# A two-block sequence model: state-space inputs scaled where they are turned, no GpSimd arithmetic beside the chunks, step sums two products later

## The chip, the cores and the metric

The kernel runs on one core of a Trainium2 chip. A core has TensorE (matmul, PE below), VectorE (DVE), ScalarE (ACT), GpSimd (POOL) and SyncE (SP), which issues most transfers. The five run their own instruction queues in order and wait for one another by semaphores. The metric is the device time of one execution in microseconds (us); lower is better.

## The reference

Two blocks follow each other on x of 1024 tokens by 1024 channels, float32. The first (a gated linear recurrence beside differential attention, then 16 experts) is not touched. The second is:

```
h    = layer_norm(x)
proj = h @ w_in      # split: xs (1024), z (1024), B (256), C (256), dt (16), glu (2048), cgate (1024)
xs, B, C = silu(causal_conv4(...));  dt = softplus(dt + bias);  a = -exp(a_log)
# state space in 8 chunks of 128 tokens, 16 heads of 64, state 128, a_cs = cumsum(dt*a) in the chunk
y_diag = ((C B^T) * exp(segment sums of dt*a, causal)) @ (xs*dt)
state  = prev*exp(a_cs[-1]) + B^T @ (xs*dt*exp(a_cs[-1]-a_cs))
y      = y_diag + exp(a_cs) * (C @ prev) + d_skip * xs
y_ssm  = group_rms(y * silu(z)) * g
y_conf = silu(layer_norm(causal_conv31(glu_a * sigmoid(glu_b)))) * silu(cgate)
h1  = layer_norm(alpha*h + [y_ssm, y_conf] @ w_out + b_out)
out = layer_norm(alpha*h1 + sigmoid(h1 @ w_ple_gate) * (p @ w_ple_proj))
```

## The kernel before

Every large product is made of three matmuls on float32r parts: a value is split into a high part (a cast on ScalarE) and a low part (a subtraction, `split`, L127 to L134), and `mm3` (L140, L141, L143) adds high*high, low*high and high*low in PSUM.

**Input projection of the second block** (`in_proj2`). Channels lie on partitions, tokens along the row. `proj` (L1247) makes one product of 128 channels by 1024 tokens in a PSUM tile `big` (three of them) and then calls `after()`, which runs what earlier steps put off in the list `later`. The order is glu(0), glu(1), B, glu(2), C, dt, glu(3), xs(0), glu(4), xs(1), ... glu(7), z(0), z(1). A glu step makes two products, forms `u` (L1343) and queues the 31-tap convolution: ten taps go to ScalarE and GpSimd (`side`), the rest to VectorE (`tap`, L1298), given out in portions of so many microseconds by `bg`. An xs step makes two products; `xbc` runs their 4-tap convolution (three VectorE instructions, L1353) and a SiLU (L1354), and one product later `turn` transposes the result to token rows in a `big` tile and `store` (L1375) copies it to SBUF by ScalarE (L1377) and stores it to the DRAM tensor `xsd`.

**The steps.** `dts` makes the product for dt; behind the next product `steps` (L1395) transposes it, takes the softplus by a chain of small VectorE instructions on [128,128] (`log1p`, L180 to L189) and forms adt = -dt*exp(a_log) (L1413). It puts `sums` (L1418) into `later`, so that its two matmuls (L1420) stand in TensorE's queue behind the product after that: they give the cumulative sums, from which `ddt` = dt*exp(total - cumulative), `cdec` and `eacs` come.

**Chunks.** `load(c)` brings token rows of `xs` and of silu(z) (`sz`); `decays(c)` forms for four heads at a time V = U*adt (U a triangle of ones) in a high part VH on VectorE and a low part VL (on GpSimd for the first VP = 2 chunks, L1654, then on ScalarE, L1658), a matmul for the segment sums, an Exp, and M = Exp*(C B^T masked) (L1661). `chunk(c)` forms xdt = xs*dt on VectorE (L1669), xdd = xs*ddt and xs*d_skip on GpSimd (L1671, L1672), the carried part po = C @ prev (L1676), y = po*eacs (L1679), xs += y on GpSimd (L1680), the state product (L1684) and its update (L1689, L1690), 16 head products M @ xdt (L1693), adds xs (L1695), multiplies by sz (L1696), takes the group norm and stores to `xsd`.

Beside chunk c runs `conf_half(c-1)` (L1592): the second half of the output product for 128 tokens. Its activations are loaded (yc) and split (low part on GpSimd); the residual `rs` = layer_norm(x)*lg + bo is made by VectorE (L1598) and GpSimd (L1599, L1600), and VectorE adds the product (L1606). Half of that product's weights is split on GpSimd, half on VectorE (L1713). The last stage, `finish`, makes the other half of the output product, the layer norms and the gate.

**Order.** The program is written in steps; a planner with costs of its own decides at build time where each instruction stands in its engine's queue (VH of a later chunk stands between instructions of the norm of an earlier one), and it fixes the waits. On the chip the queues run in that order.

Of the kernel before, what the change touches and what calls it, by code (L numbers as in the profile page):

```python
# [9 lines left out]
F = mybir.dt.float32  # L10
# [3 lines left out]
AF = mybir.ActivationFunctionType  # L14
# [25 lines left out]
LINE = 512  # L40
EDGE = 352
ZM = 3
VP = 2


_COLS = [
# [66 lines left out]
class Core:  # L113
# [1054 lines left out]
    def phase_c(self, es0):  # L1168
        nc, tc, I = self.nc, self.tc, self.I
        d = lambda n, s: tc.dram_tile(s, F, name=n)  # L1170
        self.ucd = d("ucd", [D, S])
        self.szd = d("szd", [S, D])
        self.xsd = d("xsd", [S, D])
        self.ycd = d("ycd", [D, S])
        self.ptd = d("ptd", [S, D])
        self.bgq, self.bgt = [], 0.0
        es = ExitStack()
        pool = lambda **k: es.enter_context(Even(tc, reuse_waits="tile", side="right", **k))
        cs1 = pool(name="cs1", bufs=1)
        self.lnm = cs1.tile([P, NB], F, name="lnm")  # L1180
        self.lnr = cs1.tile([P, NB], F, name="lnr")
        pool = lambda **k: es.enter_context(Even(tc, reuse_waits="tile", side="right", **k))
        self.ph = pool(name="hT2", bufs=1)
        self.cl_es = ExitStack()
        cl = self.cl_es.enter_context(Even(tc, name="cl", bufs=1, reuse_waits="tile", side="right"))
        self.BT = cl.tile([P, 2, S], F, name="BT")
        self.CT = cl.tile([P, 2, S], F, name="CT")
        self.Bk = cl.tile([P, NB, 256], F, name="Bk")
        nb = [P, NB, NE]
        self.dt = cl.tile(nb, F, name="dt")  # L1190
        self.adtH, self.adtL = (cl.tile(nb, R, name="adt" + n) for n in "HL")
        self.ddt = cl.tile(nb, F, name="ddt")
        self.eacs = cl.tile(nb, F, name="eacs")
        self.cdec = cl.tile(nb, F, name="cdec")
        self.in_proj2(cl)
        self.mix(es)

    def in_proj2(self, cl):
# [58 lines left out]
        def first(w):  # L1257

            x0, *n0 = self.x0
            turned(0, x0)  # L1260
            with tc.issue_after(self.last.ins):
                x1, *n1 = self.normed(1, [self.cf.tile([P, S + 30], F, name="u", bufs=3)[:, 0:D] if i < 3 else
                                          self.cf.tile([P, S], F, name="acc", bufs=3) for i in range(4)])
            pss = []
            for half in range(2):
                hs = slice(half * 512, half * 512 + 512)
                if half:
                    turned(1, x1)
                    for i, (mv, r) in enumerate((n0, n1)):
                        nc.vector.tensor_copy(self.lnm[:, i * 4:i * 4 + 4], mv[:, :, 0])  # L1270
                        nc.vector.tensor_copy(self.lnr[:, i * 4:i * 4 + 4], r)
                pss.append(pq.tile([P, S], F, name="big"))
                for kt in range(KT):
                    for j in range(2):
                        self.mm3([pss[half][:, j * 512:j * 512 + 512]], w[kt][0][:, j * P:(j + 1) * P],
                                 w[kt][1][:, j * P:(j + 1) * P], [hH[kt][:, hs]], [hL[kt][:, hs]], kt == 0, kt == KT - 1)
            return pss
# [94 lines left out]
        def xs(jj):  # L1372
            w = weights(W[:, jj * 256:(jj + 1) * 256])

            def store(j, pt):  # L1375
                o = st.tile([P, NB, P], F, name="t2")
                nc.scalar.copy(o, pt)  # L1377
                nc.sync.dma_start(self.xsd[:, j * P:(j + 1) * P].rearrange("(b p) c -> p b c", p=P), o)

            for i in range(2):  # L1380
                j = jj * 2 + i
                t = ct(1)
                xbc(j, proj(w, i), t)
                later.append(lambda j=j, t=t: turn(t, lambda pt: store(j, pt)))
                self.bg(7.0)

        def dts():
            self.dsk = cl.tile([P, NE], F, name="dsk")
            self.row_bcast(self.dsk, "d_skip")
            ps = proj(weights(W[:, 2560:2576]), 0, NE)  # L1390
            raw = st.tile([NE, S], F, name="t2")
            nc.scalar.activation(raw, ps[0:NE, :], AF.Identity, bias=self.col("dt_bias")[0:NE])
            later.append(lambda: steps(raw))

        def steps(raw):  # L1395

            pt = pq.tile([P, NB, P], F, name="big")
            for b in range(NB):
                nc.tensor.transpose(pt[:, 0, b * NE:(b + 1) * NE], raw[:, b * P:(b + 1) * P], self.ident[0:NE, 0:NE])
            cut = Cut(sm.tile([P, S], F, name="cut"))  # L1400
            v = cut.tile([P, P], F, "v")
            nc.scalar.copy(v, pt[:, 0])
            e = cut.tile([P, P], F, "e")
# [23 lines left out]
                nc.scalar.activation(f(self.cdec), tot, AF.Exp)  # L1427
                nc.scalar.activation(f(self.eacs), pt[:, 0], AF.Exp)

            later.append(sums)  # L1430

        def z_weights(q):
            return weights(W[:, 1024 + q * 256:1280 + q * 256])
# [137 lines left out]
    def mix(self, es):  # L1571

        nc, tc, I = self.nc, self.tc, self.I
        es2 = ExitStack()
        pool = lambda **k: es2.enter_context(Even(tc, reuse_waits="tile", **k))
        st = pool(name="yst", bufs=2)
        p0 = pool(name="y0", bufs=1)
        pqs = ExitStack()
        pq = pqs.enter_context(Even(tc, name="ypq", bufs=1, space=PSUM, reuse_waits="tile"))
        lg = p0.tile([P, D], F, name="lg")  # L1580
        bo = p0.tile([P, D], F, name="bo")
        ws = self.ws

        def begin():
            self.row_bcast(lg, "ln_emb_g")
            self.row_bcast(bo, "b_out")
            lb = st.tile([P, D], F, name="rs")
            self.row_bcast(lb, "ln_emb_b")
            nc.scalar.mul(lg, lg, ALPHA)
            nc.vector.scalar_tensor_tensor(bo, lb, ALPHA, bo, op0=ALU.mult, op1=ALU.add)  # L1590

        def conf_half(b):  # L1592
            sl = slice(b * P, (b + 1) * P)
            yc = st.tile([P, KT, P], F, name="yc")
            nc.sync.dma_start(yc, self.ycd[:, sl].rearrange("(k p) t -> p k t", p=P))
            rs = st.tile([P, D], F, name="rs")
            nc.sync.dma_start(rs, self.x1d[sl, :])
            nc.vector.tensor_scalar(rs, rs, self.lnm[:, b:b + 1], self.lnr[:, b:b + 1], op0=ALU.subtract, op1=ALU.mult)  # L1598
            nc.gpsimd.tensor_mul(rs, rs, lg)  # L1599
            nc.gpsimd.tensor_add(rs, rs, bo)  # L1600
            aH = st.tile([P, D], R, name="aH")
            aL = st.tile([P, D], R, name="aL")
            self.split(aH, aL, yc.rearrange("p k t -> p (k t)"), nc.gpsimd)
            ps = pq.tile([P, D], F, name="big")
            self.rows_product(ps, aH, aL, ws)
            nc.vector.tensor_add(rs, ps, rs)  # L1606
            nc.gpsimd.dma_start(self.ptd[sl, :], rs)

        begin()
        self.ssd(conf_half)  # L1610
        self.raw2 = pool(name="w2r", bufs=4)
        self.finish(es2, pqs, st, p0, conf_half)
        es2.close()
        es.close()

    def ssd_open(self):
# [12 lines left out]
        def load(c):  # L1629
# [3 lines left out]
            dq.dma_start(xs, self.xsd[sl, :])  # L1633
            sz = st.tile([P, D], F, name="sz")
            dq.dma_start(sz, self.szd[sl, :])
            return xs, sz

        def decays(c):

# [2 lines left out]
            for g in range(2):  # L1642
# [5 lines left out]
                for q in range(2):  # L1648
                    h0 = g * 8 + q * 4
                    sg = pseg.tile([P, 512], F, name="seg")  # L1650
                    for i, a in enumerate((self.adtH, self.adtL)):
                        V = st.tile([P, 4, P], R, name="V" + "HL"[i])
                        if i == 0 or c < VP:
                            (nc.gpsimd if i else nc.vector).tensor_mul(V, self.U[:, None, :].to_broadcast([P, 4, P]),  # L1654
                                                 a[:, c, h0:h0 + 4, None].to_broadcast([P, 4, P]))
                        else:
                            for j in range(4):
                                nc.scalar.activation(V[:, j], self.U, AF.Copy, scale=a[:, c, h0 + j:h0 + j + 1])  # L1658
# [4 lines left out]
                Ms.append(Mg)  # L1663
            return Ms

        def chunk(c, xs, sz, Ms, psum):
            sl = slice(c * P, (c + 1) * P)
            xdt = st.tile([P, D], F, name="xdt", bufs=1)
            nc.vector.tensor_mul(h16(xdt), h16(xs), bc(self.dt, c))  # L1669
            xdd = st.tile([P, D], F, name="xdd", bufs=1)  # L1670
            nc.gpsimd.tensor_mul(h16(xdd), h16(xs), bc(self.ddt, c))  # L1671
            nc.gpsimd.tensor_mul(h16(xs), h16(xs), self.dsk[:, :, None].to_broadcast([P, NE, 64]))  # L1672
            if c > 0:
                po = psum("y")
                for g in range(2):
                    nc.tensor.matmul(po[:, g * 512:(g + 1) * 512], self.CT[:, g, sl], prev[:, g * 512:(g + 1) * 512],  # L1676
                                     start=True, stop=True)
                y = st.tile([P, D], F, name="y", bufs=1)
                nc.vector.tensor_mul(h16(y), h16(po), bc(self.eacs, c))  # L1679
                nc.gpsimd.tensor_add(xs, xs, y)  # L1680
            if c < NB - 1:
                ps = psum("s")
                for g in range(2):
# [23 lines left out]
    def ssd_first(self, pq):  # L1707
# [2 lines left out]
        nx = []  # L1710

        def weights():
            self.ws = self.out_weights(self.ph, 1, None, (self.nc.gpsimd, self.nc.vector))  # L1713

        def ahead():
            nx.append(self.decays(0))
# [217 lines left out]
```

## Time and profile before

| | us |
|---|---|
| median of 3 runs (lowest, highest) | 2306.09 (2303.46, 2309.35) |
| profiled execution | 2310.75 |
| its span, first to last instruction | 2308.9 |
| TensorE busy | 2089.4 (90%) |
| VectorE busy | 1810.7 (78%) |
| ScalarE busy | 1197.2 (52%) |
| GpSimd busy | 743.5 (32%) |

The mean granted TensorE clock of the execution is 0.95 of full speed. The second block's input projection with its convolutions lies between about 1370 and 1850 us of the span, the chunks with the first half of the output product between 1850 and 2082, the last stage behind them. Times in rows are from the span's start. A row's `<-` names what it read, or, behind an idle time, what the engine waited for. TensorE's busy time counts matmuls that overlap in the array once.

### The profile page before, as it was taken

How to read it: one execution, taken by the hardware profiler on the slowest of the kernel's cores; microseconds unless marked ns; L12 is line 12 of the kernel's file. 1: busy time of each engine (PE TensorE's matmuls, PEld its weight loads, DVE VectorE, ACT ScalarE, POOL GpSimd, SP SyncE). 2: the span in 40 equal slices, each digit the busy share in tenths (PEclk: the TensorE clock that was granted, in tenths of full speed). 3: DMA queues.
4: the chain of work that ended last, by engine and by line, in shares of the span. 5: the costliest groups of instructions: out<-in, count | busy, mean ns of one | idle time of the engine just before them, and what ended most of it. 6: DMA issues, size and time to landing. Idle time of an engine off the chain costs nothing. (4 is left out here: it accounts for less than half of the span.)

```text
span 2308.9 us, 26964 instructions
## 1 busy us (share of the span) xinstructions
PE 2089.4 (90%) x10158; PEld 1717.0 (74%) x10158; DVE 1810.7 (78%) x2341; ACT 1197.2 (52%) x1403; POOL 743.5 (32%) x344
## 2 busy tenths in 40 slices
PE   4899899988979999998999599699999987997997
PEld 3677678877868888876788478478898876676885
DVE  8677859977878988987788739968864678986676
ACT  5474839872327777766677546435544342444111
POOL 2324310130022132212131129747762276653000
PEclk8899999998979999999999799899999988999998
DMA  7434455216579999998997411222234463346211
GB/s 262 146 123 133 119 148 108 101 50 230 188 275 337 381 379 394 374 346 299 322 376 295 128 47 37 64 72 65 91 112 159 150 207 103 121 162 210 82 64 64
DMA packets 213858, 422.89 MB, mean 183 GB/s; under 512 B 46144, under 2 KB 118080, under 8 KB 213600
## 3 DMA queue, kind: packets, MB, share of 16 engines
q1 hardware_dynamic: 198528, 380.27, 47.1%
q0 software_dynamic: 9440, 34.61, 4.9%
q10 hardware_dynamic: 5760, 6.29, 0.8%
q8 instruction: 80, 1.31, 0.2%
q14 instruction: 50, 0.41, 0.1%
HBM read 362.35 MB, written 58.77 MB: 182 GB/s over the span
## 5 line engine op out<-in xcount | busy, mean ns | idle before, releaser
L130 ACT CAST wH<-wr 128x2048 fp32r<-128x2048 f32 (+1 forms) x262 | 438.2, 1678 | 243.9 <-PE big L143 159.7
L134 DVE TENSOR_TENSOR wL<-wr,wH 128x2048 fp32r<-128x2048 f32 (+1 forms) x197 | 463.3, 2369 | 82.5 <-ACT wH L130 81.2
L140 PE MATMUL big<-hH,wH 128*128 128x512 f32 (+1 forms) x720 | 283.3, 399 | 10.9 <-ACT B L410 3.7
L141 PE MATMUL big<-hL,wH 128*128 128x512 f32 (+1 forms) x720 | 286.3, 399 | 7.1 <-DVE hL L326 6.1
L134 POOL TENSOR_TENSOR wL<-wr,wH 128x1024 fp32r<-128x1024 f32 (+2 forms) x66 | 164.3, 2497 | 272.8 <-ACT wH L130 252.4
L143 PE MATMUL big<-hH,wL 128*128 128x512 f32 (+1 forms) x720 | 228.5, 395 | 0.0
L1298 DVE SCALAR_TENSOR_TENSOR tr<-u,cols,tr 128x1024 f32<-128x1024 f32 x160 | 205.7, 1285 | 17.7 <-ACT tr L1286 14.2
L1295 POOL TENSOR_TENSOR acc<-acc,tmp 128x1024 f32<-128x1024 f32 x72 | 173.1, 2406 | 33.3 <-ACT tmp L1294 29.5
L140 PEld LDWEIGHTS big<-hH,wH 128*128 128x128 f32 (+1 forms) x720 | 135.9, 189 | 44.2 <-ACT hH L324 4.3
L140 PE MATMUL big<-hH,aH 128*128 128x512 f32 x384 | 157.1, 410 | 10.3 <-DVE rs L1606 4.9
L141 PEld LDWEIGHTS big<-hL,wH 128*128 128x128 f32 (+1 forms) x720 | 137.0, 190 | 39.2 <-DVE hL L326 6.4
L143 PEld LDWEIGHTS big<-hH,wL 128*128 128x128 f32 (+1 forms) x720 | 136.2, 189 | 31.4 <-issue 0.9
L140 PE MATMUL big<-wH,0H 128*128 128x512 f32 x384 | 152.6, 397 | 3.7 <-ACT 0H L130 3.7
L141 PE MATMUL big<-wL,1H 128*128 128x512 f32 x384 | 153.7, 400 | 2.3 <-DVE wL L134 2.3
L141 PE MATMUL big<-hL,aH 128*128 128x512 f32 x384 | 154.8, 404 | 0.4 <-DVE hL L1559 0.4
L141 PE MATMUL big<-wL,0H 128*128 128x512 f32 x384 | 154.1, 401 | 0.0
L140 PE MATMUL big<-wH,1H 128*128 128x512 f32 x384 | 151.5, 395 | 2.0 <-ACT 1H L130 2.0
L1005 POOL DMA_INDIRECT xe<-h2d,idx x16 | 43.3, 2708 | 340.0 <-issue 252.2
L140 PE MATMUL big<-wH,hH 128*128 128x256 f32 (+1 forms) x448 | 150.4, 336 | 1.7 <-ACT B L410 1.7
L141 PE MATMUL big<-wL,hH 128*128 128x256 f32 (+1 forms) x448 | 148.9, 333 | 0.0
L143 PE MATMUL big<-wH,hL 128*128 128x256 f32 (+1 forms) x448 | 148.4, 332 | 0.0
L143 PE MATMUL big<-wH,1L 128*128 128x512 f32 x384 | 120.5, 395 | 7.6 <-DVE 1L L134 7.6
(541 smaller groups left out, 4812.3 us busy)
## 6 DMA issues: line engine op xcount, KB each, us to landing
wr<-in_w_dram SPq DMA_DIRECT2D x192, 1024.0 KB, 8.0
wr<-in_w_in_dram SPq DMA_DIRECT2D x48, 512.0 KB, 4.3
wm<-in_w_mod_dram SPq DMA_DIRECT2D x32, 512.0 KB, 3.8
wm<-in_w_mod_dram SPq DMA_DIRECT2D x8, 1024.0 KB
wr<-in_w_in_dram SPq DMA_DIRECT2D x32, 256.0 KB, 3.0
u<-ucd SPq DMA_DIRECT2D x16, 512.0 KB, 4.1
wr<-in_w_out_dram SPq DMA_DIRECT2D x14, 512.0 KB, 5.6
xt<-in_x_dram SPq DMA_DIRECT2D x12, 512.0 KB, 9.1
```

The costliest lines, as they stand in the source:

```text
L130: self.high = nc.scalar.copy(h, src)
L134: (le or nc.vector).tensor_sub(l, src, h)
L140: mm(o, aH, bH, start=start, stop=False)
L141: mm(o, aH, bL, start=False, stop=False)
L143: mm(o, aL, bH, start=False, stop=stop)
L1005: nc.gpsimd.indirect_dma_start(out=xe, out_offset=None, in_=self.h2d, in_offset=bass.IndirectOffsetOnAxis(ap=idx[:, :1], axis=0))
L1295: nc.gpsimd.tensor_add(part[0], part[0], tmp)
L1298: nc.vector.scalar_tensor_tensor(acc[0], u[:, t:t + S], w(t), acc[0], op0=ALU.mult, op1=ALU.add)
```

## The change

`store` no longer copies: it multiplies the turned tile in PSUM by d_skip, by dt and by ddt, three VectorE products with a broadcast, and stores each to a DRAM tensor of its own (`xsd`, `xdtd`, `xddd`); the chunks load all three. As `ddt` must be there by then, `sums` is put into `later` by way of one more product. In the chunks the carried part is scaled in PSUM and added to xs by VectorE; VL is ScalarE's in all chunks. Of the output product's first half, L1598 becomes a ScalarE activation with scale and bias (the bias, -mean*rstd, is formed once in `lnb`), and the two operations on `rs`, the low part of yc and the weights' low parts go from GpSimd to VectorE. The scratch `cut` of the steps moves to the tile `t1`, and `t2` has three buffers.

```
             def store(j, pt):
-                o = st.tile([P, NB, P], F, name="t2")
-                nc.scalar.copy(o, pt)
-                nc.sync.dma_start(self.xsd[:, j * P:(j + 1) * P].rearrange("(b p) c -> p b c", p=P), o)
+
+                v = pt.rearrange("p b (h c) -> p b h c", c=64)
+                hs = slice(2 * j, 2 * j + 2)
+                for dst, f in ((self.xsd, self.dsk[:, None, hs, None].to_broadcast([P, NB, 2, 64])),
+                               (self.xdtd, self.dt[:, :, hs, None].to_broadcast([P, NB, 2, 64])),
+                               (self.xddd, self.ddt[:, :, hs, None].to_broadcast([P, NB, 2, 64]))):
+                    o = st.tile([P, NB, P], F, name="t2", bufs=3)
+                    nc.vector.tensor_mul(o.rearrange("p b (h c) -> p b h c", c=64), v, f)
+                    nc.sync.dma_start(dst[:, j * P:(j + 1) * P].rearrange("(b p) c -> p b c", p=P), o)
...
-            cut = Cut(sm.tile([P, S], F, name="cut"))
+            cut = Cut(ct(1))
...
-            later.append(sums)
+            later.append(lambda: later.append(sums))
...
-            nc.vector.tensor_scalar(rs, rs, self.lnm[:, b:b + 1], self.lnr[:, b:b + 1], op0=ALU.subtract, op1=ALU.mult)
-            nc.gpsimd.tensor_mul(rs, rs, lg)
-            nc.gpsimd.tensor_add(rs, rs, bo)
+            nc.scalar.activation(rs, rs, AF.Identity, bias=self.lnb[:, b:b + 1], scale=self.lnr[:, b:b + 1])
+            nc.vector.tensor_mul(rs, rs, lg)
+            nc.vector.tensor_add(rs, rs, bo)
...
-            self.split(aH, aL, yc.rearrange("p k t -> p (k t)"), nc.gpsimd)
+            self.split(aH, aL, yc.rearrange("p k t -> p (k t)"))
...
+            xdt = st.tile([P, D], F, name="xdt")
+            dq.dma_start(xdt, self.xdtd[sl, :])
+            xdd = st.tile([P, D], F, name="xdd", bufs=1)
+            dq.dma_start(xdd, self.xddd[sl, :])
+            return xs, sz, xdt, xdd
...
-                        if i == 0 or c < VP:
-                            (nc.gpsimd if i else nc.vector).tensor_mul(V, self.U[:, None, :].to_broadcast([P, 4, P]),
+                        if i == 0:
+                            nc.vector.tensor_mul(V, self.U[:, None, :].to_broadcast([P, 4, P]),
...
-            xdt = st.tile([P, D], F, name="xdt", bufs=1)
-            nc.vector.tensor_mul(h16(xdt), h16(xs), bc(self.dt, c))
-            xdd = st.tile([P, D], F, name="xdd", bufs=1)
-            nc.gpsimd.tensor_mul(h16(xdd), h16(xs), bc(self.ddt, c))
-            nc.gpsimd.tensor_mul(h16(xs), h16(xs), self.dsk[:, :, None].to_broadcast([P, NE, 64]))
...
-                y = st.tile([P, D], F, name="y", bufs=1)
-                nc.vector.tensor_mul(h16(y), h16(po), bc(self.eacs, c))
-                nc.gpsimd.tensor_add(xs, xs, y)
+                nc.vector.tensor_mul(h16(po), h16(po), bc(self.eacs, c))
+                nc.vector.tensor_add(xs, po, xs)
...
-            self.ws = self.out_weights(self.ph, 1, None, (self.nc.gpsimd, self.nc.vector))
+            self.ws = self.out_weights(self.ph, 1, None, (self.nc.vector, self.nc.vector))
```

## Rows read from the trace of the kernel before

**Rows 1.** Windows: stretch, its length, busy time of each engine (instructions), clock, DMA share, GB/s

```profile
1467.35:1478.70 11.35, 11.35 (x56) 9.50 (x56) 9.13 (x10) 5.26 (x7) 6.82 (x3) 1.00 0.06 15
1478.90:1501.20 22.30, 0.22 (x1) 0.02 (x1) 22.17 (x26) 8.85 (x9) 12.01 (x6) 0.61 0.13 37
1599.61:1644.95 45.34, 45.34 (x210) 37.69 (x209) 36.20 (x31) 24.62 (x23) 33.48 (x15) 1.00 0.27 82
1873.40:2064.00 190.60, 161.34 (x697) 123.17 (x696) 175.53 (x191) 75.28 (x180) 130.35 (x62) 0.88 0.42 142
1969.10:1990.50 21.40, 19.43 (x97) 15.62 (x98) 20.95 (x25) 10.50 (x27) 13.87 (x8) 1.00 0.38 128
1990.50:2015.10 24.60, 22.04 (x96) 17.57 (x95) 22.86 (x31) 9.67 (x27) 15.72 (x9) 0.86 0.35 124
```

**Rows 2.** TensorE's waits, 1400 to 1700 us: total, times, longest

```profile
PE big L1420 <- DVE cut L1413: 22.1, 1, 22.1
```

**Rows 3.** TensorE's waits in the chunks, 1873.4 to 2064.0 us

```profile
PE y L1693 <- DVE M L1661: 9.5, 8, 2.3
PE seg L1644 <- DVE M L1661: 6.8, 2, 4.9
PE big L140 <- DVE rs L1606: 4.7, 3, 2.5
PE seg L1659 <- DVE M L1661: 2.5, 1, 2.5
PE seg L1659 <- POOL VL L1654: 2.2, 1, 2.2
PE seg L1659 <- DVE cbm L1646: 2.2, 1, 2.2
```

**Rows 4.** Timelines of VectorE and GpSimd: start, duration, engine, line, instruction

```profile
2045.90 3.03 DVE L1654 TENSOR_TENSOR VH<-iota,adtH 128x512 fp32r<-128x512 f32 x1
2046.01 2.37 POOL L1680 TENSOR_TENSOR xs<-xs,y 128x1024 f32<-128x1024 f32 x1
...
2050.59 0.68 DVE L1654 TENSOR_TENSOR VH<-iota,adtH 128x512 fp32r<-128x512 f32 x1
```

**Rows 5.** VectorE's groups, 1873.4 to 2064.0 us: busy us, mean ns, idle before

```profile
L1654 DVE TENSOR_TENSOR VH<-iota,adtH 128x512 fp32r<-128x512 f32 x26 | 46.8, 1804 | 0.0
...
L1669 DVE TENSOR_TENSOR xdt<-xs,dt 128x1024 f32<-128x1024 f32 x7 | 14.6, 2088 | 5.6 <-DMA xs<-xsd 5.6
L1689 DVE TENSOR_TENSOR prev<-prev,cdec 128x1024 f32<-128x1024 f32 x6 | 13.6, 2258 | 0.0
L134 DVE TENSOR_TENSOR hL<-wr,hH 128x1024 fp32r<-128x1024 f32 x4 | 9.5, 2392 | 0.0
L173 DVE SCALAR_TENSOR_TENSOR sry<-srt,sry 128x2 f32<-128x2 f32 x18 | 9.3, 518 | 0.6
L171 DVE TENSOR_TENSOR srt<-sry 128x2 f32<-128x2 f32 x18 | 8.1, 453 | 0.4
...
L1598 DVE TENSOR_SCALAR rs<-rs,lnm,lnr 128x1024 f32<-128x1024 f32 x8 | 7.1, 891 | 0.0
...
L172 DVE SCALAR_TENSOR_TENSOR srt<-srt,srv 128x2 f32<-128x2 f32 x18 | 2.8, 157 | 0.5
```

**Rows 6.** The product that reads PSUM, by its line: ns least/median/most, first and last start

```profile
L1679 DVE TENSOR_TENSOR y<-y,eacs x7: 1207/1217/1219, 1903.8 to 2065.9; 128x1024 f32<-128x1024 f32 x7
```

**Rows 7.** VectorE's timeline while xs is turned, idle before in brackets

```profile
1554.27 2.51 DVE L1343 SCALAR_TENSOR_TENSOR u<-t,t 128x1024 f32<-128x1024 f32 x1 [13.82 <-ACT t L1338]
...
1599.61 2.51 DVE L1343 SCALAR_TENSOR_TENSOR u<-t,t 128x1024 f32<-128x1024 f32 x1 [6.36 <-ACT t L1338]
...
1604.43 1.29 DVE L1298 SCALAR_TENSOR_TENSOR tr<-u,cols,tr 128x1024 f32<-128x1024 f32 x1 [2.19 <-ACT tr L1286]
```

**Rows 8.** ScalarE's groups, 1300 to 2309 us

```profile
L1658 ACT ACTIVATE VL<-iota,adtL 128x128 fp32r<-128x128 f32 x96 | 30.3, 388 | 0.0
...
L1148 ACT ACTIVATE t<-t,nm,cer 128x1024 f32<-128x1024 f32 x2 | 2.5, 1240 | 0.5 <-DVE nm L1145 0.5
```

More of the change, by code (lines that the diff above doesn't have):

```diff
@@ L42 @@
 ZM = 3
-VP = 2
 _COLS = [
@@ L1172, in phase_c @@
         self.szd = d("szd", [S, D])
-        self.xsd = d("xsd", [S, D])
+        self.xsd, self.xdtd, self.xddd = d("xsd", [S, D]), d("xdtd", [S, D]), d("xddd", [S, D])
         self.ycd = d("ycd", [D, S])
@@ L1181, in phase_c @@
         self.lnr = cs1.tile([P, NB], F, name="lnr")
+        self.lnb = cs1.tile([P, NB], F, name="lnb")
         pool = lambda **k: es.enter_context(Even(tc, reuse_waits="tile", side="right", **k))
@@ L1271, in first @@
                         nc.vector.tensor_copy(self.lnr[:, i * 4:i * 4 + 4], r)
+                    nc.vector.scalar_tensor_tensor(self.lnb, self.lnm, -1.0, self.lnr, op0=ALU.mult, op1=ALU.mult)
                 pss.append(pq.tile([P, S], F, name="big"))
@@ L1390, in dts @@
             ps = proj(weights(W[:, 2560:2576]), 0, NE)
-            raw = st.tile([NE, S], F, name="t2")
+            raw = st.tile([NE, S], F, name="t2", bufs=3)
             nc.scalar.activation(raw, ps[0:NE, :], AF.Identity, bias=self.col("dt_bias")[0:NE])
@@ L1635, in load @@
             dq.dma_start(sz, self.szd[sl, :])
-            return xs, sz
+            xdt = st.tile([P, D], F, name="xdt")
[3 more added lines that the diff above has]
+            return xs, sz, xdt, xdd
         def decays(c):
@@ L1664, in decays, with chunk @@
             return Ms
-        def chunk(c, xs, sz, Ms, psum):
+        def chunk(c, xs, sz, xdt, xdd, Ms, psum):
             sl = slice(c * P, (c + 1) * P)
-            xdt = st.tile([P, D], F, name="xdt", bufs=1)
-            nc.vector.tensor_mul(h16(xdt), h16(xs), bc(self.dt, c))
-            xdd = st.tile([P, D], F, name="xdd", bufs=1)
-            nc.gpsimd.tensor_mul(h16(xdd), h16(xs), bc(self.ddt, c))
-            nc.gpsimd.tensor_mul(h16(xs), h16(xs), self.dsk[:, :, None].to_broadcast([P, NE, 64]))
             if c > 0:
```

## The prediction

> **What bounds the kernel now.** I read the page first (TensorE is busy for 90% of the span, so what can be gained is its waits and its slow clock), then the busy time by stretches, then who TensorE waits for in two stages, and last the single VectorE instructions there.
>
> In the input projection, TensorE is full in a steady glu and xs period of 45.34 us: 45.34 busy at clock 1.00, VectorE 36.20 [rows 1]. There is one hole. Between 1478.90 and 1501.20 TensorE is busy for 0.22 us [rows 1]: the matmuls of `sums` stand in its queue directly behind one product and wait 22.1 us for `adt` (L1413) [rows 2].
>
> The chunks (1873.4 to 2064.0) look different: 190.60 us, TensorE 161.34 at a mean granted clock of 0.88, VectorE 175.53, GpSimd 130.35 [rows 1]. TensorE's six longest kinds of wait add to 9.5 + 6.8 + 4.7 + 2.5 + 2.2 + 2.2 = 27.9 us, all but one of them on VectorE, 18.8 on M [rows 3]. VectorE is late because its instructions are stretched. The same VH product takes 0.68 us alone and 3.03 us when GpSimd's L1680, begun 0.11 us later, runs beside it [rows 4]; its mean over 26 is 1804 ns [rows 5]. The product that reads PSUM (L1679) takes 1207 to 1219 ns in all seven, GpSimd or not [rows 6]. So GpSimd stretches VectorE instructions whose operands lie in SBUF, and not those that read PSUM. The period of 21.40 us is what the stage can do when TensorE keeps clock 1.00; the next one takes 24.60 at 0.86 [rows 1].
>
> **The sums (L1430).** `sums` moves from behind the second product after the steps to behind the third. A product is at most 11.35 us (that row holds one and eight tiny turns) [rows 1], I take 11.0. TensorE does the first xs product in the hole and then waits about 22.1 - 11 = 11 us: **-11.0**. The chain of small VectorE instructions does not begin earlier, so the wait does not vanish. Bounds: nothing if the chain ends later by as much, because the xs product's own convolution taps get in front of it; -22.1 if the chain also became shorter.
>
> **The turned inputs (L1376).** One ACT copy per block goes, and three VectorE products and three 512 KB stores come. The form is L1679's (PSUM times a broadcast, into SBUF): 1.22 us [rows 6]. 8 blocks x 3 x 1.22 = 29.3 us on VectorE, 7.3 per period of two blocks. The period leaves VectorE 6.36 + 2.19 = 8.55 us idle [rows 7], so it fits with 1.2 to spare. It does not fit in the first period: the 13.82 us that VectorE idles at 1540 to 1554 [rows 7] shrink by the 11.0 that TensorE is earlier and by 7.3 of products, which leaves 4.5 too little. `u` is then late, with it the next taps, and the turn on TensorE that waits for their SiLU. **+4**, between 0 (the turn is put behind other matmuls) and 29.3 (every product exposed). The stores leave by SP's queue, the weight loads queue behind them; the stage's DMA share is 0.27 [rows 1], and 16 more half-megabyte stores over eight products' time are covered by it. `cut` and the third `t2` change places in memory, at no cost: the buffer of `t1` that `cut` now holds is wanted only by the second xs block, after `sums`.
>
> [...]
>
> **The chunks.** VectorE loses the stretch: VH 26 x (1.804 - 0.68) = 29.2; xdt 7 x (2.088 - 1.22) = 6.1; prev 6 x (2.258 - 1.22) = 6.2; hL 4 x (2.392 - 1.22) = 4.7; the small ones 18 x (0.518 + 0.453 - 2 x 0.16) = 11.7 (0.16 is what L172, of the same shape, takes) [rows 5]. Together 57.9. It also loses xdt itself (7 x 1.22 = 8.5) and L1598 (7.1) [rows 5]. It gains what GpSimd did: 16 on rs, 8 aL, about 7 sums of po and xs, 4 splits of the output weights, 35 x 1.22 = 42.7. Net -31: 175.5 becomes about 144. GpSimd's other instructions (xdd, the skip product) were made earlier or are gone.
>
> ScalarE takes L1598 (1.24 us by the Identity with scale and bias, L1148) and the low V of chunks 0 and 1: 8 x 1.24 + 32 x 0.388 = 22 us [rows 8] beside 75.28 of 190.60 busy [rows 1]: covered. Two more loads per chunk add 8.4 MB to about 27 (142 GB/s over 190.6 us) [rows 1]; with a shorter stage the DMA share goes from 0.42 to some 0.64: covered, as xdt has two buffers and no longer waits for the store and reload of `xs` (5.6 us in one chunk [rows 5]). `xdd` has one buffer: its load waits on SP for the state product of the chunk before, and behind it stand the next half's yc and x1d loads. The next state product wants it a whole period (21.4 us at best) later, and that covers it; if the cover goes, every us that yc comes late is a us of TensorE's. PSUM `y` is held by two VectorE operations instead of one (+1.2 us per chunk); other matmuls lie between.
>
> What does TensorE get? Nothing at least, and at most both losses: 27.9 of waits and 0.12 x 190.6 = 22.9 of clock, 51. The nearest row is the period of 21.40: seven of them instead of 190.6 would give 41, but the first holds chunk 0's start and the output weights' splits. VectorE's 144 must fit too. I take half of both, **-26**: a stage of 164.6 us, VectorE 87% busy.
>
> Sum: -11 + 4 - 26 = -33 from the profiled execution's 2310.75 (span 2308.9, 1.85 around it): 2277.8. That execution lies 4.7 above the median 2306.09; from the median it is 2273. I say **2275**.
>
> **Rivals.**
> (a) *VectorE's queue becomes the bound.* The order of each queue is fixed when the program is built. If the planner puts three taken-over operations (two on rs, one on aL) in front of an M that TensorE waits for, each of eight chunks pays 3.6 us (29), which eats the 26; and if the products in the turning stage stand in front of the convolution's taps, all 29 are exposed. -11 + 29 - 26 + 29 = +21: 2327. It decides from about 3 us of wait on M per chunk more than remains otherwise. For it: M is already what TensorE waits for, and the turning stage has only 1.2 us to spare. Against: VectorE is 31 us freer in the chunks.
> (b) *Hidden anyway.* Relief on VectorE only exposes the chain of state, M and output product, and the period stays near 24: -7 for the chunks, -11 + 4: 2292. Against: a 21.40 period exists with VectorE 20.95 busy.
> (c) *Both losses go.* TensorE runs through at clock 1.00, down to what VectorE allows: -44 for the chunks, and the turning stage costs nothing: 2306 - 55 = 2251. Against: VectorE's 144 would then fill 98% of the stage's 146.6.
> (d) *It doesn't do what it says:* `sums` moves and the chain of small operations moves with it, the stretch has another cause, and all stays as it is: 2306. Against: [rows 4].
>
> **How the numbers follow.** Forecast 0.55 (its own range 2262 to 2289); (a) 0.12, (b) 0.17, (c) 0.11, (d) 0.05. 0.3% is 6.9 us, about what a measurement of this kernel can tell from no change. Faster: 0.55 + 0.11 + most of (b) 0.12 = 0.78; the same: the rest of (b) and (d), 0.10; slower: (a), 0.12. Range 2251 to 2304: it leaves out (a), and what lies beyond (c).
>
> **What would show it.** `sums` waits about 11 us instead of 22.1. VH at 0.68 us throughout, waits on M halved, granted clock in the chunks above 0.93, periods of 21 to 22 us. The turn of xs waits for its SiLU by a few us in all. Wrong would be: waits on M as before with VH clean (the order, rival a), TensorE no longer full in the glu and xs periods, or waits for yc or xdd loads.

## The result, and the profile after

The changed kernel takes **2272.57 us** (median of 4 runs, 2269.55 to 2273.93) against 2306.47 (4 runs of the same occasion): ratio 0.9845, 95% interval 0.983 to 0.9861, about 34 us or 1.5% faster. The forecast was 2275. The sum came out, its terms did not. Three parts of the span show it, for all kernels of this document. The *projection* runs from the start of u of glu(3) (L1344; L1343 in the kernel before) to the start of the last Tanh of z(3) (L1460; L1453). The *chunks* run from there to the later of two starts: the last product with sz (L1701; L1696) and the last sum into rs (L1613; L1606). The *last stage* is what follows. The first 1484 us belong to none of the three.

| us of the profiled execution | projection | chunks | last stage | span |
|---|---|---|---|---|
| before | 389.7 (1485.03 to 1874.73) | 205.9 (to 2080.63) | 228.3 | 2308.9 |
| after | 390.1 (1483.80 to 1873.85) | 169.1 (to 2042.96) | 227.6 | 2270.6 |

The whole gain lies in the chunks. The projection gained nothing, though `sums` stands one product later than in the kernel before.

The windows of the kernel after (columns as in [rows 1]): one period of glu and xs, then the chunks; the second fence is the same stretch of the chunks in the kernel before.

```profile
1593.61:1641.31 47.70, 45.55 (x210) 37.62 (x209) 42.78 (x36) 22.79 (x21) 35.62 (x15) 1.00 0.43 121
1873.85:2042.96 169.11, 163.22 (x782) 129.90 (x781) 138.82 (x227) 88.39 (x199) 7.98 (x15) 0.96 0.63 218
```

```profile
1874.73:2080.63 205.90, 176.39 (x775) 135.48 (x773) 185.45 (x216) 77.68 (x187) 132.54 (x64) 0.89 0.42 142
```

The period is 2.36 us longer than in [rows 1] and TensorE is no longer full in it. In the chunks VectorE lost 46.6 us, GpSimd does nothing but issue transfers (8 us), and TensorE's own busy time fell by 13 as its mean granted clock rose from 0.89 to 0.96.

TensorE's waits of the kernel after, from 1400 to 1850 us and then in the chunks (total, times, longest):

```profile
PE big L1427 <- DVE t L1420: 12.5, 1, 12.5
PE big L1361 <- ACT t L1355: 10.0, 4, 3.6
```

```profile
PE y L1698 <- issue: 3.2, 1, 3.2
PE seg L1670 <- DVE M L1672: 1.6, 1, 1.6
PE big L139 <- DVE rs L1613: 0.4, 1, 0.4
PE big L139 <- DVE xs L1701: 0.2, 1, 0.2
```

Against [rows 2] the wait of `sums` lost 9.6 us, and four turns of xs now wait 10.0 us for their SiLU (one turn and 1.9 us before). Against [rows 3] the 18.8 us of waits on M in the chunks are 1.6.

VectorE's groups in the chunks of the kernel after, to be held against [rows 5, 6] (busy us, mean ns, idle before):

```profile
L1665 DVE TENSOR_TENSOR VH<-iota,adtH 128x512 fp32r<-128x512 f32 x26 | 17.5, 684 | 1.4 <-PE seg L1670 1.4
...
L1684 DVE TENSOR_TENSOR y<-y,eacs 128x1024 f32<-128x1024 f32 x7 | 8.6, 1223 | 1.0 <-PE y L1682 1.0
...
L1694 DVE TENSOR_TENSOR prev<-prev,cdec 128x1024 f32<-128x1024 f32 x6 | 7.3, 1213 | 0.0
...
L170 DVE TENSOR_TENSOR srt<-sry 128x2 f32<-128x2 f32 x21 | 3.3, 158 | 0.5
L172 DVE SCALAR_TENSOR_TENSOR sry<-srt,sry 128x2 f32<-128x2 f32 x21 | 3.3, 158 | 0.5
```

VH falls from 1804 to 684 ns, prev*cdec from 2258 to 1213, the small steps of the root from 518 and 453 to 158. The product that reads PSUM (L1684) is unchanged: 1223 against 1217.

### The profile page after: what moved, and what is told of

It is laid out like the page before. It is cut to its first block, busy times and chain, and to the rows that moved or that the text cites. A ratio compares the mean times of both kernels' runs of the same rounds, so it can differ in the third digit from the quotient of the medians.

```text
span 2270.6 us, 27059 instructions
## 1 busy us (share of the span) xinstructions
PE 2080.1 (92%) x10158; PEld 1712.4 (75%) x10158; DVE 1787.8 (79%) x2385; ACT 1210.0 (53%) x1437; POOL 607.8 (27%) x287
## 4 chain that ended last, share of the span: by engine, by line
PE 58%; DVE 6%; ACT 3%; issue 2%; DMA 2%; POOL 0%; SPq 0%; ACTq 0%; DVEq 0%; POOLq 0%
PE big L142 17%; PE big L140 17%; PE big L139 17%; PE y L1698 1%; DVE wL L133 1%; PE tr L1012 1%; ACT wH L129 1%; DMA x1d<-y,idx 1%; DVE tr L1299 1%; PE tr L997 1%; PE seg L1670 1%; DVE aL L133 0%; PE big L1361 0%; PE y L1682 0%; ACT aH L129 0%
## 5 line engine op out<-in xcount | busy, mean ns | idle before, releaser
L142 PE MATMUL big<-hH,aL 128*128 128x512 f32 x384 | 124.7, 399 | 3.0 <-DVE aL L133 2.7
```

Source lines behind the costliest of these rows:

```text
L142: mm(o, aL, bH, start=False, stop=stop)
```

## The experiments

Each time is the median of 4 to 6 runs; the kernel before took 2306.8 to 2307.3 us beside them. The three parts are those of the profiled execution, which lies up to 3.4 us off the median. "Conv first" below is the kernel of e4, and e5 to e9, e11 and e12 are built on it.

| | us | ratio (95%) | projection | chunks | last stage |
|---|---|---|---|---|---|
| e1 after, `sums` early | 2272.0 | 0.9844 (0.9826 to 0.9861) | 397.2 | 161.0 | 225.4 |
| e2 after, rs and aL on GpSimd | 2265.8 | 0.982 (0.9806 to 0.9834) | 390.2 | 162.9 | 225.0 |
| e3 after, scaled in the chunks | 2283.6 | 0.9891 (0.9876 to 0.9905) | 377.6 | 193.8 | 226.8 |
| e4 after, conv first | 2253.5 | 0.9767 (0.9752 to 0.9781) | 377.8 | 164.1 | 224.9 |
| e5 conv first, GpSimd as busy as before | 2283.3 | 0.9896 (0.9879 to 0.9912) | 377.8 | 196.8 | 223.9 |
| e6 conv first, 112 idle products | 2280.3 | 0.9884 (0.9868 to 0.99) | 378.3 | 185.8 | 226.8 |
| e7 conv first, `sums` three later | 2251.0 | 0.9757 (0.9743 to 0.977) | 376.8 | 162.9 | 224.3 |
| e8 conv first, `sums` early | 2262.8 | 0.9811 (0.9794 to 0.9827) | 390.9 | 163.4 | 226.3 |
| e9 conv first, 49 idle products | 2268.2 | 0.9838 (0.9819 to 0.9857) | 378.3 | 174.5 | 230.4 |
| e10 before, `sums` later | 2292.1 | 0.9931 (0.9913 to 0.9949) | 377.2 | 201.4 | 228.2 |
| e11 e7, eacs first | 2251.0 | 0.9757 (0.9736 to 0.9778) | 376.3 | 162.7 | 224.8 |
| e12 e11, rs and aL on GpSimd | 2251.0 | 0.9764 (0.9745 to 0.9783) | 376.2 | 161.9 | 226.4 |

**e1: `sums` back in its old place.**

```
-            later.append(lambda: later.append(sums))
+            later.append(sums)
```

> The kernel after, with `sums` put back behind the second product after the steps; nothing else is undone. Theory (order in VectorE's queue): TensorE's waits for the SiLU of xs (10.0 us, four of them) come from the three products of one block standing in VectorE's queue ahead of the next block's convolution, wherever `sums` stands. Then the wait of `sums` returns (12.5 becomes about 22), the four waits stay at 2 us each in the steady periods, and the time is about 2272.6 + 9 = 2281. Rival (time on VectorE): the turned products eat what `sums` gave, because VectorE has no time left once TensorE runs ahead. Then the later start of TensorE gives VectorE that time back, the waits for SiLU vanish, and the time stays at 2272 to 2274.

2272.0, the rival's number, and yet not by the rival's way: the wait is 22.1 again and the turns still wait 8.4 in all, as the theory said, and the projection is 7.1 us longer. What pays it back is the chunks, 8.1 us shorter with unchanged code. The planner laid out another order there (VectorE's instructions differ from the 41st of the stage on), and the kernel after loses time at one place of its own order. First two pieces of its chain of work that ended last, then VectorE's instruction there, then the windows up to the wait's end and behind it:

```profile
1991.27 3.20 issue
1994.47 6.87 PE y L1698 x32
```

```profile
1993.15 1.22 DVE L1685 TENSOR_TENSOR xs<-y,xs 128x1024 f32<-128x1024 f32 x1
```

```profile
1972.59:1994.88 22.29, 19.08 (x89) 14.72 (x89) 17.16 (x30) 12.08 (x29) 1.06 (x2) 1.00 0.63 222
1994.88:2020.84 25.96, 25.96 (x110) 21.28 (x110) 19.64 (x34) 10.71 (x27) 1.06 (x2) 0.81 0.49 174
```

TensorE waits 3.2 us ahead of a chunk's head products. The profile names no releaser ("issue"). But the head products write the one PSUM buffer `y`, which holds the carried part until L1685 has read it, and they start 0.1 us after L1685 ends; in e3 the profile names the same sum for 5.9 us of such a wait. Behind the wait the granted clock is 0.50 from 1994.6 to 2004.6, and the 32 matmuls of the head products take 6.87 us instead of 3.68. By my estimate ten us at that clock cost 5 (10.0 x 0.50); with the 3.2 of the wait that is about the whole 8.1. That the wait brought the slow clock on is not shown: the trace has the one behind the other. In e1's chunks there is no such wait, the clock is 0.99 and not 0.96, and TensorE is busy for 157.7 us and not 163.2.

The end of the chunks differs too. The matmuls with the last chunk (output product left out), first of the kernel after, then of e1:

```profile
2037.97 3.68 PE L1698 MATMUL y<-xdt,M 128*128 128x64 f32 x32
2041.49 1.04 PE L1772 MATMUL tr<-ident,yc 128*128 128x128 f32 x8
2044.28 1.06 PE L1772 MATMUL tr<-ident,yc 128*128 128x128 f32 x8 [1.75 <-issue]
```

```profile
2034.07 3.68 PE L1698 MATMUL y<-xdt,M 128*128 128x64 f32 x32
2043.25 1.97 PE L1772 MATMUL tr<-ident,yc 128*128 128x128 f32 x16 [1.32 <-DVE rs L1613]
```

In the kernel after, the last head products stand behind the whole output product, and nothing is left to run beside the norm that follows; in e1 some 4 us of the output product follow them (2037.6 to 2041.9). The last stage is 2.2 us shorter in e1. That this place is the reason was not tested. The later runs with ready-made inputs and no idle products (e2, e4, e7, e8, e11, e12) have chunks of 161.9 to 164.1 us at a clock of 0.99.

**e4: the second block's convolution ahead of the first block's three products.**

```
-                nc.vector.scalar_tensor_tensor(a[:, k:S], ...
+                self.conv = nc.vector.scalar_tensor_tensor(a[:, k:S], ...
...
+            pend = []
             for i in range(2):
...
                 xbc(j, proj(w, i), t)
-                later.append(lambda j=j, t=t: turn(t, lambda pt: store(j, pt)))
+                if i == 0:
+                    later.append(lambda j=j, t=t: turn(t, lambda pt: pend.append((j, pt))))
+                else:
+                    with tc.issue_after(self.conv.ins):
+                        store(*pend.pop())
+                    later.append(lambda j=j, t=t: turn(t, lambda pt: store(j, pt)))
```

`issue_after` puts what is issued under it behind that instruction, here the convolution's last.

> The kernel after, with the three products of an xs step's first block put behind the convolution of its second block in VectorE's queue (they are the same 24 products; nothing is taken out). Theory (order in VectorE's queue): the second block's convolution begins about 3.3 us earlier, its SiLU is done before TensorE wants it, and the four waits go: the period of glu and xs falls from 47.70 to about 45.6 us, the time by 6 to 10 us to 2263 to 2267. Against it: the turned tile holds its PSUM buffer some 8 us longer, and TensorE may wait for that instead. Rival (time on VectorE): the queue is full whichever comes first, what is put behind is late in its turn, and the time stays at 2271 to 2274.

2253.5, 19 us faster than the kernel after and beyond the theory: 12.3 come from the projection, 5.0 from the chunks, where the slow place named under e1 is gone, and 2.7 from the last stage. The reason for the 12.3 stands in VectorE's timeline. The kernel after, one period from 1593.61, and then e4, one period from 1585.83:

```profile
1614.72 1.22 DVE L1384 TENSOR_TENSOR t<-big,dsk 128x1024 f32<-128x1024 f32 x1
1615.86 1.21 DVE L1384 TENSOR_TENSOR t<-big,dt 128x1024 f32<-128x1024 f32 x1
1616.99 1.21 DVE L1384 TENSOR_TENSOR t<-big,ddt 128x1024 f32<-128x1024 f32 x1
1618.12 1.28 DVE L1299 SCALAR_TENSOR_TENSOR tr<-u,cols,tr 128x1024 f32<-128x1024 f32 x1
1619.31 1.27 DVE L1354 SCALAR_TENSOR_TENSOR t<-big,cols,t 128x1023 f32<-128x1023 f32 x1
...
1624.07 1.27 DVE L1354 SCALAR_TENSOR_TENSOR t<-big,cols,t 128x1021 f32<-128x1021 f32 x1
...
1641.31 1.33 DVE L1344 SCALAR_TENSOR_TENSOR u<-t,t 128x1024 f32<-128x1024 f32 x1 [2.24 <-ACT t L1339]
```

```profile
1607.71 1.28 DVE L1354 SCALAR_TENSOR_TENSOR t<-big,cols,t 128x1023 f32<-128x1023 f32 x1
...
1612.48 1.28 DVE L1354 SCALAR_TENSOR_TENSOR t<-big,cols,t 128x1021 f32<-128x1021 f32 x1
1613.67 1.22 DVE L1384 TENSOR_TENSOR t<-big,dsk 128x1024 f32<-128x1024 f32 x1
1614.80 1.22 DVE L1384 TENSOR_TENSOR t<-big,dt 128x1024 f32<-128x1024 f32 x1
1615.93 1.22 DVE L1384 TENSOR_TENSOR t<-big,ddt 128x1024 f32<-128x1024 f32 x1
```

In the kernel after, the convolution of the period's second block begins 25.7 us into the period, behind the first block's three products; in e4 it begins at 21.9. Its SiLU is then done before TensorE asks for the turn, the four waits are gone, and the period is [rows 1]'s 45.34 again, with VectorE 41.65 busy. The one new wait, 0.3 us, is on ScalarE (L1333), so the turned tile's longer stay in PSUM costs next to nothing.

**e10, e8, e7: where `sums` stands, on other orders.** e10 is the kernel before with e1's edit the other way round; e8 is e4 with e1's edit.

> The kernel before, with `sums` put behind one more product and nothing else changed. Theory: the wait of 22.1 us becomes 12.5 and nothing gives it back, since VectorE has no turned products there: 2306.5 - 9.6 = 2297, range 2294 to 2300. Rival (the next period gives it back, as it does in the kernel after): 2304 to 2307.

> The same kernel with the convolution first (2253.5), and `sums` put back where the kernel before had it. It closes the square of two places of `sums` by two orders of VectorE's queue. Theory (in the changed order the turned products gave the wait of `sums` back; with the order mended they can't): the wait is 22 again and the time is about 9.6 longer, 2261 to 2264. Rival (the wait of `sums` is hidden anyway, whatever the order): 2252 to 2255.

e8 came out (2262.8). e10 went the theory's way and beyond its range: 2292.1 against 2294 to 2300. Without the turned products the move shortens the projection by 12.5 (e10 against before): 9.6 are the wait of `sums`, 1.9 the turn that no longer waits. (The chunks, whose code is the same, came out 4.5 shorter; the medians differ by 15.2.) In the mended order the move is worth 13.1 (e8 against e4), and in the changed order 7.1 (e1 against after). So the turned products cost the kernel after 390.05 - 377.22 = 12.8 us of projection against e10: 10.0 of waits, and 2.8 of TensorE's busy time (367.5 against 364.7 us). In the mended order they cost 0.5.

e7 puts `sums` one product later still:

```
-            adt = cut.tile([P, P], F, "adt")
+            adt = f(self.eacs)
...
-                tot = cut.tile([P, P], F, "tot")
+                tot, e = f(self.cdec), f(self.ddt)
...
-            later.append(lambda: later.append(sums))
+            later.append(lambda: later.append(lambda: later.append(sums)))
```

> The same kernel with the convolution first (2253.5), and `sums` behind one more product (three in all against the kernel before the change's one; adt, the total and the exponent live in the tiles of eacs, cdec and ddt). Theory: the wait of 12.5 us becomes 1 to 2 us, but the first turned tile then waits for its SiLU, whose convolution stands in VectorE's queue behind the chain of steps, for about 5: net -5, range -11 to -2, 2242 to 2251. Rival (TensorE that comes earlier only waits in the next period, as in the run with `sums` early): nothing, 2253.

TensorE's waits of e7, from 1400 to 1850 us:

```profile
PE big L1361 <- ACT t L1355: 4.8, 1, 4.8
PE big L139 <- ACT eacs L1441: 4.8, 1, 4.8
PE big L1433 <- DVE eacs L1426: 1.8, 1, 1.8
```

The 12.5 us became 1.8, and two waits of 4.8 took their place, of which one was foreseen: 1.0 us of projection, the lowest time so far but not apart from e4's (the intervals overlap). e11 issues the exponential for eacs first:

> The run with `sums` three products later (2251.0), with the exponential for eacs issued right behind the copy of the totals. There TensorE waited 4.8 us for a PSUM buffer that this exponential, the last reader of the sums, held. Theory: that wait goes down to 1 or 2 us, the time to 2247 to 2249. Rival (the wait for the first turned tile's SiLU, 4.8 us, takes it over, or the queue puts the exponential where it was): 2250 to 2252.

The wait for the buffer went from 4.8 to 3.7 us (its last reader is now ddt), the time did not move: the rival.

**e2, e3: which part made the gain of the chunks.** e2 gives the three operations per 128 tokens on rs and yc back to GpSimd:

```
-            nc.vector.tensor_mul(rs, rs, lg)
-            nc.vector.tensor_add(rs, rs, bo)
+            nc.gpsimd.tensor_mul(rs, rs, lg)
+            nc.gpsimd.tensor_add(rs, rs, bo)
...
-            self.split(aH, aL, yc.rearrange("p k t -> p (k t)"))
+            self.split(aH, aL, yc.rearrange("p k t -> p (k t)"), nc.gpsimd)
```

> The kernel after, with only the output product's three operations per 128 tokens (rs times lg, rs plus bo, low part of yc) back on GpSimd: 24 instructions of some 2.4 us, 58 us beside the chunks, where the kernel before had 134 there; xdt, xdd and the scaled xs stay loaded ready-made, VectorE gets 24 x 1.22 = 29 us freer. Theory (GpSimd stretches VectorE's instructions in SBUF): VH is stretched again where they overlap (mean 0.69 us becomes 1.1 to 1.4), waits on M come back, the clock falls again; of the 41 us of the chunks some 58/134 x 41 = 18 return: 2290, range 2280 to 2300. Rival (the gain came from inputs that need no arithmetic in the chunk): nothing returns, with VectorE freer at most 2273.

My theory missed: 2265.8. VH was stretched as foretold (mean 963 ns), but VectorE was rid of 29 us of work at the same time, its busy time stayed at 134.6, and the chunks took 162.9. (Of the 6.8 us against the kernel after, 6.2 lie in the chunks, where the slow place named under e1 is missing: clock 0.99.) e3 takes the ready-made inputs away (one copy by ScalarE and one store per turned tile, as before) and leaves GpSimd idle:

```
+            nc.vector.tensor_mul(h16(xdt), h16(xs), bc(self.dt, c))
+            nc.vector.tensor_mul(h16(xdd), h16(xs), bc(self.ddt, c))
+            nc.vector.tensor_mul(h16(xs), h16(xs), self.dsk[:, :, None].to_broadcast([P, NE, 64]))
```

> The kernel after, with the scaling by skip, step and decayed step done in the chunks again, but all three on VectorE (24 products of 1.22 us, 29 us); the turned tile is copied by ScalarE and stored once, as before; no GpSimd arithmetic beside the chunks. Theory (GpSimd's absence made the gain): the chunks hold most of it; VectorE has 137.9 + 29 = 167 us of work in a stage that took 166.4, so it becomes the bound and the stage gets 10 to 20 us longer (177 to 186, against 207 before), while the four waits for the SiLU of xs go (-8 to -10): 2272.6 + 15 - 9 = 2279, range 2270 to 2287. Rival (the ready-made inputs made the gain): the chunks are back near 200 and the time at 2272.6 + 35 - 9 = 2299 or above.

The time, 2283.6, lies in the theory's range; the stage, 193.8, lies nearer the rival's 200. So neither taking GpSimd out alone, with its work on VectorE (205.9 to 193.8), nor, as e5 shows next, the ready-made inputs alone make the 42.

**e5, e6, e9: GpSimd that nobody waits for.** In e6 and e9 GpSimd multiplies constants into a scratch tile beside the chunks; e5 has 12 such products per chunk, e2's edit, and half of the weights' low parts and the low V of chunks 0 and 1 on GpSimd.

```
+            if b < NB - LAG:
+                for q in range(16):      # e9: 7
+                    qs = slice(q % 4 * 256, q % 4 * 256 + 256)
+                    nc.gpsimd.tensor_mul(idle, lg[:, qs], bo[:, qs])
```

> The kernel of the run before this one that puts the convolution first (2253.5), with as much GpSimd arithmetic beside the chunks as the kernel before had (132 us): the three operations per 128 tokens on rs and yc, half of the weights' low parts and the low V of chunks 0 and 1 are GpSimd's again, and in place of the three products that the ready-made inputs replaced (xdd, the skip product, the sum of the carried part) GpSimd makes products of constants that nobody reads (84 of 128x256 in all). The inputs stay ready-made. Stage of the chunks = end of z(3) to the later of the last chunk and the last rs sum: before 205.9, scaled in the chunks on VectorE alone 193.8, conv first 164.1. Theory (the ready-made inputs made most of the gain: VectorE has slack that can take GpSimd's stretch, as 59 us of GpSimd cost nothing): the stage takes 164 to 174, the time 2253 to 2264. Rival (GpSimd's arithmetic was what cost, from some amount on): the stage goes back to 190 or more, the time to 2280 or more.

> The same kernel with the convolution first (2253.5); GpSimd makes 112 products of constants (128x256, 16 beside each of seven chunks, some 70 us) that nobody reads, everything else as it was. It measures contention by itself, without a dependence. Theory (VectorE has slack): VectorE's instructions in SBUF are stretched (VH from 0.685 to 1.0 or more), its busy time rises from 137 to 155 or more, and the stage of 164.1 grows by 0 to 8: 2253 to 2262. Rival (contention reaches TensorE directly): each us of stretch is a us of the stage, 20 us or more: 2273.

> The kernel with the convolution first (2253.5); GpSimd makes 49 products of constants (128x256, 7 beside each of seven chunks) that nobody reads, against 112 in the run that took 2280.3. At 0.94 us each GpSimd is busy for 46 us more, and VectorE by 25.6 x 46 / 105 = 11 us: 148 instead of 137. Theory (the stage follows VectorE's busy time, by whatever it is raised, about one us per us once it is over TensorE's): the runs so far have 137 us and a stage of 164, and 162 to 163 us and 186 to 194; at 148 it is 172 to 176, the time 2261 to 2266. Rival (slack up to TensorE's own 158 us, and a loss only behind that): the stage stays at 164 to 167, the time at 2253 to 2257.

The windows of the chunks, in this order: e4, e9, e6, e5, e3.

```profile
1861.34:2025.44 164.10, 158.26 (x774) 124.50 (x773) 137.19 (x227) 89.46 (x203) 7.48 (x14) 0.99 0.65 222
```

```profile
1861.65:2036.13 174.48, 165.11 (x782) 130.66 (x781) 148.63 (x226) 88.29 (x199) 56.16 (x64) 0.95 0.61 211
```

```profile
1863.05:2048.82 185.77, 167.79 (x782) 131.83 (x781) 162.75 (x227) 88.53 (x199) 113.10 (x127) 0.94 0.58 198
```

```profile
1860.83:2057.65 196.82, 169.15 (x775) 128.38 (x773) 167.78 (x200) 86.65 (x195) 145.49 (x127) 0.93 0.54 184
```

```profile
1862.91:2056.75 193.84, 170.29 (x783) 133.24 (x781) 160.58 (x245) 88.65 (x199) 8.02 (x15) 0.92 0.46 153
```

Read the length against VectorE's busy time, the third of the busy columns. 137 goes with 164, 149 with 174, 163 with 186, 161 with 194, 168 with 197, and before 185 with 206. The stage goes with VectorE's load, whether the load is arithmetic of its own (e3), stretch by idle products (e6, e9) or both, at 0.8 to 1.3 us per us of VectorE above e4's. VectorE is nowhere full (83 to 90% of the stage): what TensorE waits for comes later. In e5 that is again M:

```profile
PE seg L1681 <- DVE M L1683: 21.1, 6, 6.0
```

The rest is TensorE's clock, 0.99 in e4 and 0.92 to 0.95 in the others: its own busy time is 6.9 (e9) to 12.0 us (e3) longer than e4's.

One reservation: the planner lays out an order of its own for each of these kernels, and e1 showed what an order can be worth. e9 and e6 are the cleanest pair, since TensorE's instructions stand in the same order in both, and VectorE's nearly so: 14.1 us more of VectorE make the stage 11.3 us longer, 0.8 per us. e4's order is another one, so that the 10.4 us from e4 to e9 may be in part the order's.

The theory's "slack" for e5 and e6 was wrong: both came out on the rival's side. (In e6 the products took GpSimd 105 us where 70 were expected, and VH came to 0.94 us, not 1.0.) e9 was made to tell slack from slope, and came out as slope (174.5 was forecast as 172 to 176; the time came 2 us above its range, in the last stage). The loss is there at 149 us of VectorE, before it reaches TensorE's 158.

e12 asked whether the lightest VectorE would make a better version:

> The run before this one of the same call (`sums` three products later, eacs first), with the three operations per 128 tokens on rs and yc on GpSimd. It asks for the best version. Theory (the stage follows VectorE's busy time only above TensorE's, and at 134 to 137 us it is below): no gain and no loss, within 3 us of the run without it. Rival (the 6.8 us that the same move gained on the kernel after are its own): 6 to 7 us faster, 2241 to 2243.

2251.0, no gain and no loss, as the theory said: at 132 to 137 us VectorE no longer sets the stage (161.9 us, 162.7 in e11). The best versions (e7, e11, e12, 2251.0, and e4 with the shortest edit, 2253.5) beat both kernels: 22 and 19 us faster than the kernel after.

## Why the prediction was right, and where its steps were wrong

- **Sums, -11.** Right in place and size: the wait fell by 9.6, and alone the move is worth 12.5 us of projection (e10). The bound "the xs product's own taps get in front of it" took 1.2 us: one such tap (L1354) stands ahead of adt.
- **Turned inputs, +4.** The mis-sized term: 12.8 (e10 against after), which ate the gain of `sums`. The step that failed is "so it fits with 1.2 to spare". In time it does fit: VectorE is busy for 42.78 of 47.70 us and still waits at u (2.24 at 1641.31, against 6.36 in [rows 7]). In order it does not: the products stand ahead of a convolution on which a turn waits. That is the order which rival (a) named for the turning stage, at 12.8 of its 29 us, and not the late u of the sum. e4 shows it: the same products one place later cost 0.5. The price of one product was right, 1.21 to 1.23 us, beside a GpSimd that is busy for 35.62 us of the period.
- **Chunks, -26.** The other mis-sized term: -36.8, and -42 where the slow place named under e1 is gone (e4). Two steps were too small. VectorE's "Net -31" is -46.6 over the chunks of the table, which are 15 us longer than the prediction's stretch. Most of the difference is the stretch of the small steps, which was counted for two of five groups: all five took 35.8 us before (86 instructions) and 12.3 after (77), where 11.7 was taken for the gain. And "half of both" had no ground: at 137 us of VectorE both losses go nearly whole, as rival (c) said (2251; e4 took 2253.5), while 149 us cost 10 us more (e9). One cover was missing: `y` held by a second VectorE operation was put at nothing ("other matmuls lie between"), and once, by all that the rows show, it cost 3.2 us of waiting, with 10 us at a granted clock of 0.50 behind them.
- **The mechanism** (GpSimd stretches VectorE's instructions with SBUF operands) was right, and e6 shows it without a dependence. VectorE's groups in its chunks:

```profile
L1676 DVE TENSOR_TENSOR VH<-iota,adtH 128x512 fp32r<-128x512 f32 x26 | 24.1, 936 | 1.1 <-PE seg L1681 1.1
L1683 DVE TENSOR_TENSOR M<-seg,cbm 128x512 f32<-128x512 f32 x28 | 18.9, 677 | 0.0
L133 DVE TENSOR_TENSOR aL<-yc,aH 128x1024 fp32r<-128x1024 f32 x8 | 11.7, 1457 | 0.0
...
L1624 DVE TENSOR_TENSOR rs<-big,rs 128x1024 f32<-128x1024 f32 x8 | 9.7, 1208 | 0.0
```

  VH and aL, with two operands in SBUF, are longer than in the kernel after (684 and 1215 ns); M and the sum into rs, which read PSUM, are not (682 and 1214). These rows show which instructions are stretched, and not what the two engines contend for. In [rows 4] VH lost 3.03 - 0.68 = 2.35 us, about the whole 2.37 of GpSimd's instruction, though VH had begun 0.11 us earlier by the trace; why it lost that much is not shown. What the prediction lacked is that such stretch cost nothing where VectorE's sum did not grow by it: in e2 VH took 963 ns in the mean and the sum was 134.6 us (138.8 in the kernel after), in e12 single ones of VH took up to 4.04 us and the sum was 132.4 (136.9 in e11).
- **Expected signs:** VH at 0.68 and waits on M gone, yes; clock above 0.93, yes (0.96); periods of 21 to 22, partly (15.1 to 26.0 from one sum into rs to the next); a wait of the turn of "a few us in all", no (10.0). One sign of being wrong came: TensorE is no longer full in the glu and xs periods (45.55 of 47.70 us).
- The last stage (-0.7) and a start 1.2 us earlier make up the rest of the 38.3 between the spans of the two profiled executions. Two errors of opposite sign, -11 and +9, gave a sum that was right to 2.4 us: the directions were foreseen, the closeness is luck.

## What to carry to other kernels

Free time on an engine does not show that new work fits there: look at what stands behind it in that queue, and who waits for that. When an engine's load sets a stage, count everything that is stretched, the tiny instructions too, and plot the stage's length against its busy time over a few variants before splitting a gain among causes. A part's price measured in one arrangement (sums: 7, 12.5 or 13 us) holds for that arrangement only. And look at the clock behind a wait of TensorE as well: 3.2 us in the kernel after were followed by 10 us at a granted clock of 0.50.

## What was not expected of the hardware

GpSimd's 128x256 product took 0.94 us beside VectorE (112 in 104.9 us), and 105 us of them stretched VectorE by 25.6 us (162.75 against 137.19): 0.24 us per us, and e9's 48 us by 11.4, as much per us. The 58 us of e12's 128x1024 operations (GpSimd's 65.64 less the 7.49 of e11, which has them on VectorE) stretched it by 132.36 - (136.90 - 24 x 1.22) = 24.7 (the busy times of e12's and e11's chunks): 0.43 per us. So the same GpSimd time cost VectorE less when it came in short pieces; but the two loads also run beside different instructions of VectorE, and that the length of the pieces is the reason is not shown. And the changes in an early stage moved later ones by up to 8 us through the order that was laid out at build time (e1): differences of that size in a stage whose code was not touched are no evidence on the edit.
